# Output projections by a Strassen scheme over 12 of 16 row tiles, in a two-layer hybrid encoder step on one core

## The chip, the core and the metric

The kernel runs on one core of a Trainium2 chip. Times are device microseconds of one execution. A core has five engines with queues of their own, worked off in order: TensorE (PE, matmuls; PEld is its weight load), VectorE (DVE), ScalarE (ACT), GpSimd (POOL) and SyncE (SP, which issues DMAs here). An instruction waits on semaphores until what it reads is written and what it overwrites has been read.

## The reference, cut to what matters

Two layers over 640 tokens (512 of a prompt, 8 x 16 of samples) with 2048 channels, all in float32:

```
h = rms_norm(x, norm_g);  z = h @ w_in
y_a = conv group (4 tiles of 128 channels), y_b = window attention (8 tiles), y_c = memory attention (4 tiles)
y = concat([y_a, y_b, y_c]) @ w_out          # 2048 x 2048, the change is here
x = x + y
```

A final RMSNorm follows the second layer.

## The kernel before, in words

Activations lie transposed: a row tile is 128 channels by 640 tokens, and there are 16 of them (`NK`). The tokens stand in two halves of 320 (`HT`). `R` [128, 16, 640] holds the outputs of the three groups, then the layer's result; rows 0 to 7 are the window attention, 8 to 11 the memory attention, 12 to 15 the convolution. `HL` [128, 32, 640] holds the matmuls' right-hand side as a high part (first 16 rows) and a low part (last 16).

A float32 product is made of three passes of a faster type: `split` writes the high part by a ScalarE copy (L126) and the low part by a VectorE subtraction (L127); a product is high x high, high x low and low x high. `x_split` does the same for a layer's input with the norm's factor in it (L129, L130). `proj` (L726 to L739) computes a column tile of a projection: 16 k tiles, three passes, two halves, 96 matmuls of 128x320 (L735) into two PSUM banks `z`. Its weights come in four chunks of 512 columns; `wprep` loads a chunk on SP's queue, splits it at high priority, and has three buffers each of `wr`, `wh` and `wl`.

A layer is 38 column tiles of w_in with the three groups' work between them, then the split of `R` into `HL` (`HL<-R`), then the column tiles of w_out: `proj`, an addition of the residual (L907), in layer 0 a store of the result to `x1d`, and `add_sq`, a square on ScalarE (L242) and a sum on VectorE (L243) for the next norm. Layer 0 does all 16 columns so. Layer 1 does 14; the last two stand in a tail of their own, in parts of 384 and 256 tokens (L931), with their weights split ahead of it into `wh` and into attention buffers (`g`, `u`).

The order on each queue is made ahead of time by a list scheduler from the program, with weight work at high priority; pools of buffers in SBUF and PSUM set which instruction waits for which reader. PSUM has two `z` tiles and four `a` tiles.

## Time and profile before

| | |
|---|---|
| Runs | 1870.96, 1871.5, 1872.04 us (median 1871.5) |
| The profiled execution's own time | 1871.64 us |
| Its span | 1869.9 us |
| TensorE busy | 1849.1 us, 99% |
| VectorE busy | 1113.7 us, 60% |
| ScalarE busy | 744.0 us, 40% |
| GpSimd busy | 159.9 us, 9% |
| Out-projections | layer 0 from 751.42 to 976.7, layer 1 from 1625.72 to 1822.84 us |

The span runs from the first to the last instruction. Busy shares are means over stages; which wait ends last is read stage by stage. TensorE's matmuls overlap, so a matmul's own duration (about 310 ns for 128x320) is longer than the distance to the next.

### The profile page before, as it was taken

How to read it: one execution, taken by the hardware profiler on the slowest of the kernel's cores; microseconds unless marked ns; L12 is line 12 of the kernel's file. 1: busy time of each engine (PE TensorE's matmuls, PEld its weight loads, DVE VectorE, ACT ScalarE, POOL GpSimd, SP SyncE). 2: the span in 40 equal slices, each digit the busy share in tenths (PEclk: the TensorE clock that was granted, in tenths of full speed). 3: DMA queues.
4: the chain of work that ended last, by engine and by line, in shares of the span. 5: the costliest groups of instructions: out<-in, count | busy, mean ns of one | idle time of the engine just before them, and what ended most of it. 6: DMA issues, size and time to landing. Idle time of an engine off the chain costs nothing.

```text
span 1869.9 us, 32663 instructions
## 1 busy us (share of the span) xinstructions
PE 1849.1 (99%) x12846; PEld 1802.2 (96%) x12846; DVE 1113.7 (60%) x2385; ACT 744.0 (40%) x1578; POOL 159.9 (9%) x349
## 2 busy tenths in 40 slices
PE   8999999999999999999999999999999999999996
PEld 8899999999998999999999999999999989999996
DVE  7859998567554445432256999756755434623235
ACT  7831224657553334322242222555654324522221
POOL 1121210000000010000021000000000010000000
PEclk9999999999999999999999999999999999999998
DMA  8844532222222343344343332222232243333333
GB/s 281 288 120 105 124 108 76 72 69 67 81 83 73 105 160 102 116 130 119 119 121 91 80 85 81 74 69 71 65 89 80 75 135 125 115 96 102 97 102 134
DMA packets 92394, 200.36 MB, mean 107 GB/s; under 512 B 12256, under 2 KB 17296, under 8 KB 92208
## 3 DMA queue, kind: packets, MB, share of 16 engines
q1 hardware_dynamic: 72592, 139.75, 24.7%
q0 software_dynamic: 17184, 55.63, 10.0%
q10 hardware_dynamic: 2464, 2.88, 0.4%
q8 instruction: 101, 1.65, 0.4%
q14 instruction: 53, 0.43, 0.1%
...
## 4 chain that ended last, share of the span: by engine, by line
PE 98%; DVE 1%; DMA 0%; ACT 0%; issue 0%; DVEq 0%; POOLq 0%
PE z L735 80%; PE a L266 3%; PE z L289 2%; PE a L483 2%; PE a L526 2%; PE a L463 2%; PE z L931 1%; DVE R L964 1%; PE a L514 1%; PE a L622 1%; PE a L661 1%; PE a L648 1%; PE a L557 1%; PE a L517 1%; PE a L595 1%; PE a L690 1%
## 5 line engine op out<-in xcount | busy, mean ns | idle before, releaser
L735 PE MATMUL z<-HL,wh 128*128 128x320 f32 x6784 | 1308.8, 311 | 0.0
L735 PEld LDWEIGHTS z<-HL,wh 128*128 128x128 f32 x6784 | 1068.8, 188 | 8.8 <-issue 5.7
L735 PE MATMUL z<-HL,wl 128*128 128x320 f32 x3392 | 788.4, 311 | 0.0
L126 ACT ACTIVATE wh<-wr 128x512 fp32r<-128x512 f32 x431 | 271.7, 631 | 761.4 <-PE z L735 682.4
L735 PEld LDWEIGHTS z<-HL,wl 128*128 128x128 f32 x3392 | 569.4, 188 | 3.5 <-issue 1.6
L127 DVE TENSOR_TENSOR wl<-wr,wh 128x512 fp32r<-128x512 f32 x431 | 297.0, 689 | 380.2 <-ACT wh L126 367.6
L411 DVE SCALAR_TENSOR_TENSOR R<-R,sm 128x128 f32<-128x128 f32 (+1 forms) x480 | 235.0, 548 | 0.1
L907 DVE TENSOR_TENSOR R<-z,zt 128x640 f32<-128x640 f32 x30 | 24.8, 825 | 70.5 <-PE z L735 70.5
L127 DVE TENSOR_TENSOR g<-a,g 128x512 fp32r<-128x512 f32 x80 | 49.5, 634 | 27.2 <-ACT g L126 26.6
L487 DVE CUSTOM_DVE_ANT_0 g<-a,R 128x256 f32<-128x256 f32 (+1 forms) x128 | 46.4, 388 | 23.4 <-PE a L483 20.0
L499 ACT ACTIVATE g<-g,sml 128x256 f32<-128x256 f32 (+1 forms) x128 | 59.8, 470 | 0.0
L126 ACT ACTIVATE g<-a 128x512 fp32r<-128x512 f32 x80 | 42.3, 552 | 42.3 <-PE a L517 29.9
L506 ACT ACTIVATE g<-g,sml 128x256 f32<-128x256 f32 (+1 forms) x128 | 51.4, 473 | 3.9 <-DVE sml L502 3.9
L471 POOL DMA_DIRECT2D R<-brep x32 | 17.4, 543 | 406.2 <-DVE sml L487 166.9
L266 PE MATMUL a<-HL,wh 128*128 128x256 f32 x256 | 42.9, 289 | 6.0 <-ACT HL L129 6.0
L127 DVE TENSOR_TENSOR wl<-u,wh 128x512 fp32r<-128x512 f32 x60 | 40.6, 687 | 6.2 <-ACT wh L126 6.1
L126 ACT ACTIVATE wh<-u 128x512 fp32r<-128x512 f32 x60 | 37.5, 627 | 15.7 <-PE z L289 8.0
L266 PEld LDWEIGHTS a<-HL,wh 128*128 128x128 f32 x256 | 37.6, 195 | 6.3 <-ACT HL L129 6.0
L289 PE MATMUL z<-wh,HL 128*128 128x512 f32 x128 | 41.1, 399 | 0.6 <-ACT wh L126 0.6
L531 ACT ACTIVATE g<-a 64x512 f32<-64x512 f32 x32 | 19.0, 594 | 41.0 <-PE a L526 40.7
L532 DVE TENSOR_TENSOR g<-a,g 64x512 f32<-64x512 f32 x32 | 22.0, 687 | 20.0 <-ACT g L531 19.6
L463 PE MATMUL a<-u,g 128*128 128x320 f32 x192 | 33.8, 312 | 0.0
...
## 6 DMA issues: line engine op xcount, KB each, us to landing
wr<-w_in SPq DMA_DIRECT2D x304, 256.0 KB, 2.7
wr<-w_out SPq DMA_DIRECT2D x128, 256.0 KB, 2.7
...
R<-xT SPq DMA_DIRECT2D x16, 320.0 KB, 5.3
zt<-xT POOLq DMA_DIRECT2D x16, 320.0 KB, 4.6
```

What stands on the lines that cost most here:

```text
L126: a = ac.activation(hi, raw, AF.Copy)
L127: v = ve.tensor_tensor(out=lo, in0=raw, in1=hi.bitcast(F32), op=ALU.subtract)
L266: pe.matmul(ps[ct][:, :256], w[:, ws], mslot(l, k, lo), start=k == 0 and n == 0, stop=k == NK - 1 and n == 2,)
L289: pe.matmul(psv[:, m, :], mslot(l, k, lo)[:, ms], w, start=k == 0 and n == 0, stop=k == NK - 1 and n == 2,)
L411: ve.scalar_tensor_tensor(out=o, in0=x, scalar=w, in1=o, op0=ALU.mult, op1=ALU.add)
L463: pe.matmul(ps[:, :HT], w[:, ws], x[:, k, :], start=n == 0, stop=n == 11)
L483: pe.matmul(ps[:, j, c0:256], q[:, p * P:(p + 1) * P], kk[n][h][:, (p - 1) * P + c0:(p + 1) * P], start=n == 0, stop=n == 1,)
L487: ve.tensor_tensor_reduce(out=x[:, j, c0:], in0=ps[:, j, c0:], in1=bt[:, c0:], scale=1.0, scalar=-3.0e38, op0=ALU.add, op1=ALU.max, accum_ ...
L499: ac.activation(x, x, AF.Exp, bias=ng[:, p:p + 1], accum_out=sm_[:, p:p + 1])
L506: ac.activation(x, x, AF.Copy, scale=rd[:, p:p + 1])
L526: pe.matmul(po[:, os], V[h][:, v, :], p[:, ms], start=v == 0 and n == 0, stop=v == 3 and n == 1, skip_group_check=True,)
L735: pe.matmul(ps[:, s, :HT], w[:, ws], HL[:, lo * NK + k, s * HT:(s + 1) * HT], start=k == 0 and n == 0, stop=k == NK - 1 and n == 2,)
```

## The change

In the out-projections, columns 0 and 1 stay as they were. The others go in pairs (j, j+1): seven pairs in layer 0 (j = 2 to 14), six in layer 1 (j = 2 to 12); the two columns of the tail stay plain. In a pair the four first row tiles (`KS`) are multiplied plainly. The other twelve are two blocks of six, `KB` (rows 4 to 9) and `KA` (rows 10 to 15); with the two halves of tokens (`TA`, `TB`) and the two columns they are a 2x2 block product, done by Winograd's form of Strassen's scheme with seven products instead of eight. A product is 6 k tiles in three passes, 18 matmuls (`s_mm`).

`combos` makes the combinations of the activations once a layer, by eight subtractions of 960 elements in `R`, and splits them into T2, T3, T4 and, over `HL`'s rows `KA` of the second half, T1. `s_pair` makes the combinations of the weights for each pair on VectorE (`s1`, `s2`, a21 becoming a11 - a21, a12 becoming a12 - s2), splits each product's weights (two buffers `sh`, `sl` of 768, six raw ones `sr`) and adds the products from the PSUM accumulators `X`, `Dd` and `z` into `R`, where the residual has been loaded (`add_to`). A pair's products come in the order p1, a12, a12 - s2, the plain part of both columns, p7, p6, p4, p5; in the last pair of layer 1 the plain part, with a12 and a12 - s2 ahead of it, comes last.

The buffers: `wr`, `wh`, `wl` and the attention buffers are in pools (`wp`, `at`) that are given back before the out-projections, whose pools (`tt`, `sw`) lie in the same memory; the tail has one more (`tw`) with weight buffers for all eight chunks. In layer 1 `R[:, KA, TB]` is stored to DRAM (`y12d`) before `combos`, and read back and split again over T1 for the tail, whose two plain columns need it. The host lays w_out out so that a column's weights are one row of 2048 a partition.

```
+    def s_mm(out, w, x, start, stop):
+        n = w[0].shape[-1] // P
+        for k in range(n):
+            for i, (a, b) in enumerate(passes(w, x)):
+                pe.matmul(
+                    out, a[:, k * P:(k + 1) * P], b[:, k, :], start=start and k == 0 and i == 0,
+                    stop=stop and k == n - 1 and i == 2, skip_group_check=True,
+                )
...
+    def combos():
...
+        T[1] = hl(KA, TB)
+        gs = [(slice(KA.start + g, KA.start + g + 3), slice(KB.start + g, KB.start + g + 3)) for g in (0, 3)]
+        for a, b in gs:
+            sub(R[:, a, TA], R[:, a, TB], R[:, a, TA])
+            sub(R[:, a, TB], R[:, b, TB], R[:, a, TB])
+            sub(R[:, b, TB], R[:, b, TB], R[:, a, TA])
+        place = {1: (0, TA), 2: (1, TB), 3: (0, TB), 4: (1, TA)}
+        for n in (3, 2, 4, 1):
+            for g, ab in enumerate(gs):
+                i, cs = place[n]
+                if n == 4:
+                    sub(R[:, ab[1], TA], R[:, ab[1], TA], R[:, ab[1], TB])
+                ks = slice(3 * g, 3 * g + 3)
+                split(R[:, ab[i], cs], None, T[n][0][:, ks, :], T[n][1][:, ks, :])
...
+    def s_pair(l, j1, T, resid, early):
...
+        for j in (j1, j2):
+            gp.dma_start(R[:, j, :], resid[j])
+        X, Dd = pa()[:, :HT], pa()[:, :HT]
+        with tc.high_priority():
+            a11 = s_load(wj[0][:, cut[0]])
+            a21 = s_load(wj[1][:, cut[0]])
+            a22 = s_load(wj[1][:, cut[1]])
+            a12 = s_load(wj[0][:, cut[1]])
+            p1 = s_split(a11)
+            s1, s2 = s_raw(), s_raw()
+            ve.tensor_tensor(out=s1, in0=a21, in1=a22, op=ALU.add)
+            sub(s2, s1, a11)
+            sub(a21, a11, a21)
+        s_mm(X, p1, hl(KA, TA), True, True)
+        add_to(R[:, j1, TA], X)
+
+        def plain():
+            z = pz()
+            with tc.high_priority():
+                w = s_split(a12)
+            s_mm(z[:, 0, :HT], w, hl(KB, TA), True, False)
+            with tc.high_priority():
+                sub(a12, a12, s2)
+                w = s_split(a12)
+            s_mm(z[:, 1, :HT], w, hl(KB, TB), True, False)
+            w = s_prep(wj[0][:, cut[2]])
+            for s, cs in enumerate((TA, TB)):
+                s_mm(z[:, s, :HT], w, hl(KS, cs), False, True)
+            add_to(half(R[:, j1, :]), z[:, :, :HT])
+            z = pz()
+            w = s_prep(wj[1][:, cut[2]])
+            for s, cs in enumerate((TA, TB)):
+                s_mm(z[:, s, :HT], w, hl(KS, cs), True, True)
+            add_to(half(R[:, j2, :]), z[:, :, :HT])
...
+        p6 = (s2, 2, X, False, [(j2, TA)])
+        p7 = (a21, 3, Dd, True, [(j2, TB)])
+        p5 = (s1, 1, X, False, [(j2, TB), (j1, TB)])
+        p4 = (a22, 4, Dd, False, [(j2, TA)])
...
+        phase_pools("tt", "sw")
         for k in range(NK):
             split(R[:, k, :], None, HL[:, k, :], HL[:, NK + k, :])
+        if l == L - 1:
+            gp.dma_start(y12d, R[:, KA, TB])
...
-    W = [(None, None)] * 3 + [(g2, g2)] * 4 + [(u5, None)]
-    W = [wprep(A["w_out"][L - 1, NK - 2 + p // 4, p % 4], *W[p]) for p in range(8)]
...
+    y12 = tl([P, 6, HT], "y12", 1, F32, cur["tw"])
+    with tc.high_priority():
+        gp.dma_start(y12, y12d)
```

In the order below, a row is a line of the program, the operation, what is written and read, and the size. VectorE where the attention of layer 0 ends, before: `wl` are low parts of weight chunks, `HL<-R` low parts of the activations; L701 is the memory attention's last product, L710 the eviction of the last w_in column.

```order
L127 TENSOR_TENSOR HL<-R,HL 128x640
L127 TENSOR_TENSOR wl_8524<-wr_8521,wh_8523 128x512
L127 TENSOR_TENSOR HL<-R,HL 128x640 x3
L652 TENSOR_TENSOR R<-a_8171,R 128x2x256
L127 TENSOR_TENSOR HL<-R,HL 128x640
L127 TENSOR_TENSOR wl_8554<-wr_8551,wh_8553 128x512
L127 TENSOR_TENSOR HL<-R,HL 128x640
L701 TENSOR_TENSOR R<-a_8354,R 128x2x64
L127 TENSOR_TENSOR HL<-R,HL 128x640 x2
L710 SCALAR_TENSOR_TENSOR zt_8480<-z_8358,rstd 128x640
L127 TENSOR_TENSOR HL<-R,HL 128x640
L127 TENSOR_TENSOR wl_8584<-wr_8581,wh_8583 128x512
```

`wl_8524`, `wl_8554` and `wl_8584` are the first three chunks of w_out. The same place after the change; `sl` are low parts of w_out's chunks, L720 is the eviction, L775 a subtraction of `combos`, L1025 and L1026 the last gate.

```order
L137 TENSOR_TENSOR HL<-R,HL 128x640 x2
L712 TENSOR_TENSOR R<-a_8361,R 128x2x64
L137 TENSOR_TENSOR HL<-R,HL 128x640 x2
L720 SCALAR_TENSOR_TENSOR zt_8487<-z_8365,rstd_1245 128x640
L137 TENSOR_TENSOR HL<-R,HL 128x640
L137 TENSOR_TENSOR sl_8539<-sr_8536,sh_8538 128x512
L137 TENSOR_TENSOR sl_8569<-sr_8566,sh_8568 128x512
L775 TENSOR_TENSOR R<-R 128x3x320
L1025 SCALAR_TENSOR_TENSOR zt_8487<-zt_8486,zt_8487 128x640
L775 TENSOR_TENSOR R<-R 128x3x320
L1026 TENSOR_TENSOR R<-R,zt_8487 128x640
L137 TENSOR_TENSOR sl_8599<-sr_8596,sh_8598 128x512
```

The first w_out chunk, `sl_8539`, has moved behind the eviction and the HL splits around it.

VectorE over one column in the middle of layer 0's out-projection, before:

```order
L907 TENSOR_TENSOR R<-z_8774,zt_8772 128x640
L127 TENSOR_TENSOR wl_8966<-wr_8963,wh_8965 128x512
L243 TENSOR_TENSOR w_1326_8517<-w_1326_8517,w_1370_8897 128x640
L127 TENSOR_TENSOR wl_8996<-wr_8993,wh_8995 128x512
L127 TENSOR_TENSOR wl_9034<-wr_9031,wh_9033 128x512
L127 TENSOR_TENSOR wl_9064<-wr_9061,wh_9063 128x512
L907 TENSOR_TENSOR R<-z_8902,zt_8900 128x640
```

After, from the end of one pair to the first plain addition of the next: `a_9319` is the last pair's `X`, `a_9569` this pair's, `sr_9577` a12, `sr_9584` s2, and L253 the sum of squares.

```order
L813 TENSOR_TENSOR R<-a_9319,R 128x320 x2
L137 TENSOR_TENSOR sl_9609<-sr_9577,sh_9608 128x768
L253 TENSOR_TENSOR w_1331_8532<-w_1331_8532,w_1461_9560 128x640
L775 TENSOR_TENSOR sr_9577<-sr_9577,sr_9584 128x768
L813 TENSOR_TENSOR R<-a_9569,R 128x320
L253 TENSOR_TENSOR w_1331_8532<-w_1331_8532,w_1462_9564 128x640
L137 TENSOR_TENSOR sl_9632<-sr_9577,sh_9631 128x768
L137 TENSOR_TENSOR sl_9656<-sr_9653,sh_9655 128x512
L137 TENSOR_TENSOR sl_9688<-sr_9685,sh_9687 128x512
L813 TENSOR_TENSOR R<-z_9607,R 128x640
```

Where a column had a weight split, an addition and a sum, the splits now stand between additions, sums and a subtraction that makes the next split's input.

VectorE where the out-projection of layer 0 ends and w_in of layer 1 begins, before: L130 are the low parts of layer 1's input, `wl` the first column of w_in.

```order
L130 SCALAR_TENSOR_TENSOR HL<-R,sm,HL 128x640 x4
L127 TENSOR_TENSOR wl_10601<-wr_10598,wh_10600 128x512
L130 SCALAR_TENSOR_TENSOR HL<-R,sm,HL 128x640 x4
L127 TENSOR_TENSOR wl_10631<-wr_10628,wh_10630 128x512
L130 SCALAR_TENSOR_TENSOR HL<-R,sm,HL 128x640 x2
L907 TENSOR_TENSOR R<-z_10438,zt_10436 128x640
L130 SCALAR_TENSOR_TENSOR HL<-R,sm,HL 128x640 x2
L127 TENSOR_TENSOR wl_10661<-wr_10658,wh_10660 128x512
```

After, the same place; `sl_10536` is the weight of p5, the last product, and `a_10319` its accumulator.

```order
L137 TENSOR_TENSOR sl_10536<-sr_10333,sh_10535 128x768
L813 TENSOR_TENSOR R<-a_10320,R 128x320
L140 SCALAR_TENSOR_TENSOR HL<-R,sm,HL 128x640 x2
L813 TENSOR_TENSOR R<-a_10319,R 128x320 x2
L140 SCALAR_TENSOR_TENSOR HL<-R,sm,HL 128x640 x2
L137 TENSOR_TENSOR wl_10613<-wr_10610,wh_10612 128x512
L137 TENSOR_TENSOR wl_10643<-wr_10640,wh_10642 128x512
L137 TENSOR_TENSOR wl_10673<-wr_10670,wh_10672 128x512
```

The first chunks of w_in, which stood among the HL splits ahead of the last addition, stand behind p5's additions and two more HL splits.

## Rows read from the trace of the kernel before

**Rows 1.** The page's first part: busy time of each engine, its share of the span, instructions.

```profile
PE 1849.1 (99%) x12846; PEld 1802.2 (96%) x12846; DVE 1113.7 (60%) x2385; ACT 744.0 (40%) x1578; POOL 159.9 (9%) x349
```

**Rows 2.** The waits of TensorE: engine, tile and line, what it waited for, microseconds in total, times, the longest.

```profile
PE a L266 <- ACT HL L129: 6.0, 1, 6.0
PE a L200 <- DVE sml L186: 2.5, 1, 2.5
PE a L210 <- ACT w L956: 1.1, 1, 1.1
PE z L289 <- ACT wh L126: 0.6, 1, 0.6
```

**Rows 3.** The page's chain that ended last, by engine and by line, in shares of the span.

```profile
PE 98%; DVE 1%; DMA 0%; ACT 0%; issue 0%; DVEq 0%; POOLq 0%
PE z L735 80%; PE a L266 3%; PE z L289 2%; PE a L483 2%; PE a L526 2%; PE a L463 2%; PE z L931 1%; DVE R L964 1%; PE a L514 1%; PE a L622 1%; PE a L661 1%; PE a L648 1%; PE a L557 1%; PE a L517 1%; PE a L595 1%; PE a L690 1%
```

**Rows 4.** Busy time by engine in a stretch of layer 0's out-projection: PE, PEld, DVE, ACT, POOL busy microseconds (instructions), TensorE's granted clock, share of the DMA engines, GB/s.

```profile
760.00:960.00 200.00, 200.00 (x1366) 200.00 (x1365) 60.08 (x84) 46.42 (x71) 15.06 (x28) 1.00 0.40 122
```

**Rows 5.** The timeline of VectorE in the same stage: start, microseconds, line, operation, idle time before it and what ended it. The additions of two successive columns.

```profile
850.18 0.82 DVE L907 TENSOR_TENSOR R<-z,zt 128x640 f32<-128x640 f32 x1 [2.46 <-PE z L735]
...
864.26 0.82 DVE L907 TENSOR_TENSOR R<-z,zt 128x640 f32<-128x640 f32 x1 [2.46 <-PE z L735]
```

**Rows 6.** The timeline of TensorE, with the pointwise projection of a convolution tile (L463) among w_in's matmuls, and where a column of the out-projection begins.

```profile
508.36 1.63 PE L463 MATMUL a<-u,g 128*128 128x320 f32 x10
509.83 0.75 PE L735 MATMUL z<-HL,wh 128*128 128x320 f32 x4
...
849.98 0.75 PE L735 MATMUL z<-HL,wh 128*128 128x320 f32 x4
```

**Rows 7.** Groups of instructions by line and shape over the whole span: count, busy microseconds, mean nanoseconds of one, idle time before them and what ended it.

```profile
L127 DVE TENSOR_TENSOR wl<-wr,wh 128x512 fp32r<-128x512 f32 x431 | 297.0, 689 | 380.2 <-ACT wh L126 367.6 <-PE z L735 9.7 <-issue 1.2
...
L243 DVE TENSOR_TENSOR w<-w,w 128x640 f32<-128x640 f32 x34 | 28.0, 825 | 5.7 <-ACT w L242 5.6
...
L426 DVE SCALAR_TENSOR_TENSOR R<-a,R 128x320 f32<-128x320 f32 x16 | 6.9, 485 | 3.9 <-PE a L191 3.7
...
L127 DVE TENSOR_TENSOR u<-R,u 128x1280 fp32r<-128x1280 f32 x4 | 6.0, 1493 | 1.7 <-PE a L463 1.6
...
L126 ACT ACTIVATE wh<-wr 128x512 fp32r<-128x512 f32 x431 | 271.7, 631 | 761.4 <-PE z L735 682.4 <-issue 48.3 <-DVE R L411 14.3
...
L242 ACT ACTIVATE w<-R 128x640 f32<-128x640 f32 x34 | 25.2, 740 | 15.6 <-DVE R L907 13.9 <-DVE w L243 1.5
```

**Rows 8.** The timelines of TensorE and of ScalarE where layer 0's out-projection begins.

```profile
751.42 0.75 PE L735 MATMUL z<-HL,wh 128*128 128x320 f32 x4
...
750.74 1.37 ACT L126 ACTIVATE HL<-R 128x640 fp32r<-128x640 f32 x2 [0.37 <-PE z L735]
752.01 0.61 ACT L126 ACTIVATE wh<-wr 128x512 fp32r<-128x512 f32 x1
```

**Rows 9.** The timeline of VectorE in the same place.

```profile
751.51 0.83 DVE L127 TENSOR_TENSOR HL<-R,HL 128x640 fp32r<-128x640 f32 x1 [0.23 <-ACT HL L126]
752.25 0.82 DVE L710 SCALAR_TENSOR_TENSOR zt<-z,rstd 128x640 f32<-128x640 f32 x1
752.99 0.81 DVE L127 TENSOR_TENSOR HL<-R,HL 128x640 fp32r<-128x640 f32 x1
753.72 0.68 DVE L127 TENSOR_TENSOR wl<-wr,wh 128x512 fp32r<-128x512 f32 x1
```

**Rows 10.** DMA issues: what is written and read, queue, count, KB each, median microseconds from issue to landing.

```profile
x1d<-R POOLq DMA_DIRECT2D x16, 320.0 KB, 3.3
...
yT<-R SPq DMA_DIRECT2D x4, 384.0 KB, 3.2
...
yT<-R SPq DMA_DIRECT2D x4, 256.0 KB, 2.5
...
o_vold<-cv POOLq DMA_DIRECT2D x1, 896.0 KB, 13.0
```

**Rows 11.** The timelines of VectorE and of ScalarE shortly before layer 1's w_in begins.

```profile
972.09 3.27 DVE L130 SCALAR_TENSOR_TENSOR HL<-R,sm,HL 128x640 fp32r<-128x640 f32 x4
...
973.83 3.02 ACT L129 ACTIVATE HL<-R,sm 128x640 fp32r<-128x640 f32 x4
```

**Rows 12.** The timelines of ScalarE and of VectorE where the tail begins.

```profile
1815.76 0.63 ACT L126 ACTIVATE wh<-wr 128x512 fp32r<-128x512 f32 x1 [2.89 <-PE z L735]
...
1823.04 0.82 DVE L907 TENSOR_TENSOR R<-z,zt 128x640 f32<-128x640 f32 x1 [1.79 <-PE z L735]
```

**Rows 13.** The timeline of TensorE at the start of the kernel; from 5.96 to 9.56 there are 17 matmuls, from 9.56 to 10.41 seven.

```profile
5.96 1.44 PE L266 MATMUL a<-HL,wh 128*128 128x256 f32 x5 [5.96 <-ACT HL L129]
...
8.68 1.04 PE L266 MATMUL a<-HL,wh 128*128 128x256 f32 x5
9.56 0.29 PE L266 MATMUL a<-HL,wl 128*128 128x256 f32 x1
...
10.41 0.76 PE L266 MATMUL a<-HL,wh 128*128 128x256 f32 x5
```

**Rows 14.** Busy time in two stretches of the tail, columns as in rows 4.

```profile
1850.00:1856.00 6.00, 4.42 (x38) 4.25 (x36) 5.93 (x15) 0.42 (x1) 0.00 (x0) 0.99 0.91 324
1856.00:1862.00 6.00, 1.22 (x4) 0.93 (x4) 5.69 (x20) 0.00 (x0) 0.00 (x0) 0.50 0.64 227
```

More of the change, by code (lines that the diff above doesn't have):

```diff
@@ L68, in build, with phase_pools @@
     dr = pool("dr", bass.MemoryType.DRAM)
-    uid, last = [0], {}
+    uid, last, cur = [0], {}, {}
+    phase = ctx.enter_context(ExitStack())
+    home = {t: "wp" for t in ("wr", "wh", "wl", "rstd")}
+    home |= {t: "at" for t in ("g2", "qh", "u5", "kc", "kh", "kl", "mh", "ml", "vh", "vl", "cqs")}
+    def phase_pools(*names):
+        phase.close()
+        for n in names:
+            uid[0] += 1
+            cur[n] = phase.enter_context(tc.tile_pool(name=f"{n}{uid[0]}", bufs=1, reuse_waits="tile"))
     def tl(shape, tag, bufs, dt=F32, pl=None):
         uid[0] += 1
-        return (pl or sb).tile(shape, dt, tag=tag, name=f"{tag}_{uid[0]}", bufs=bufs)
+        pl = pl or (cur[home[tag]] if tag in home else sb)
+        return pl.tile(shape, dt, tag=tag, name=f"{tag}_{uid[0]}", bufs=bufs)
     def w25():
@@ L301, in build @@
     mraw = []
+    phase_pools("wp", "at")
     def load_mem(j):
@@ L712, in evac2 @@
     def evac2(ps, outp, outs, scale=1.0):
+        rs3 = half(cur["rstd"])
         ve.scalar_tensor_tensor(
@@ L739, in proj, with s_raw, s_split, s_load @@
         return ps
+    KS, KB, KA = slice(0, 4), slice(4, 10), slice(10, 16)
+    TA, TB = slice(0, HT), slice(HT, TOK)
+    def s_raw(n=6):
+        return tl([P, 768], "sr", 6, F32, cur["sw"])[:, :n * P]
+    def s_split(raw):
+        n = raw.shape[-1]
+        hi = tl([P, 768], "sh", 2, F32R, cur["sw"])[:, :n]
+        lo = tl([P, 768], "sl", 2, F32R, cur["sw"])[:, :n]
+        split(raw, None, hi, lo)
+        return hi, lo
+    def s_load(src):
+        raw = s_raw(src.shape[-1] // P)
+        load(raw, src)
+        return raw
@@ new lines, in s_prep, with sub, hl @@
+    def s_prep(src):
+        with tc.high_priority():
+            return s_split(s_load(src))
+    def sub(out, a, b):
+        ve.tensor_tensor(out=out, in0=a, in1=b, op=ALU.subtract)
+    def hl(ks, cs):
+        return HL[:, ks, cs], HL[:, slice(NK + ks.start, NK + ks.stop), cs]
+    def combos():
+        T = {}
+        tt = [
+            (tl([P, 6, HT], f"th{n}", 1, F32R, cur["tt"]), tl([P, 6, HT], f"tl{n}", 1, F32R, cur["tt"]))
+            for n in (2, 3, 4)
+        ]
+        T[2], T[3], T[4] = tt
+        T[1] = hl(KA, TB)
[12 more added lines that the diff above has]
+                split(R[:, ab[i], cs], None, T[n][0][:, ks, :], T[n][1][:, ks, :])
+        return T
@@ new lines, in s_mm, with add_to, mixed @@
+    def s_mm(out, w, x, start, stop):
[6 more added lines that the diff above has]
+                )
+    def add_to(out, ps):
+        ve.tensor_tensor(out=out, in0=ps, in1=out, op=ALU.add)
+    def s_pair(l, j1, T, resid, early):
+        j2 = j1 + 1
+        wj = [A["w_out"][l, j1], A["w_out"][l, j2]]
+        cut = [slice(ks.start * P, ks.stop * P) for ks in (KA, KB, KS)]
+        for j in (j1, j2):
[31 more added lines that the diff above has]
+            add_to(half(R[:, j2, :]), z[:, :, :HT])
+        def mixed(raw, n, out, start, dst):
+            with tc.high_priority():
+                w = s_split(raw)
+            s_mm(out, w, T[n], start, True)
+            for j, cs in dst:
+                add_to(R[:, j, cs], out)
+        p6 = (s2, 2, X, False, [(j2, TA)])
+        p7 = (a21, 3, Dd, True, [(j2, TB)])
+        p5 = (s1, 1, X, False, [(j2, TB), (j1, TB)])
+        p4 = (a22, 4, Dd, False, [(j2, TA)])
+        if not early:
+            plain()
+        for a in (p7, p6, p4, p5):
+            mixed(*a)
+        if early:
+            plain()
```

56 lines of the change are left out of this document (43 added, 13 removed).

## The prediction

> **What bounds the kernel now.** I read the page's busy shares first: TensorE is busy 99% of the span, VectorE 60%, ScalarE 40% [rows 1]. Then the waits: in 1869.9 us TensorE waits four times, 10.2 us in all, none of them in the projections [rows 2]. The chain of waits says the same: 98% of it is TensorE, 80% the one matmul line of the projections [rows 3]. So the end is set by the number of matmuls times their pace, and an edit gains what it takes off TensorE's queue, less what it makes TensorE wait. In the out-projection stage the other engines have room: in a stretch of 200 us TensorE is busy for all of it, VectorE for 60 us, ScalarE for 46 [rows 4].
>
> The pace comes from the VectorE timeline: the residual additions of successive columns start 14.08 us apart [rows 5], and a column has 96 matmuls, so 146.7 ns for one of 128x320.
>
> **What is removed.** Thirteen pairs of columns (seven in layer 0, six in layer 1) go from 192 matmuls to seven products of 18 and 48 plain ones, 174. So 13 x 18 = 234 matmuls fall, and the built order of TensorE has just that many fewer. At 146.7 ns: **34.3 us**. A new product uses each weight block twice (high part), then its low block once, where `proj` uses them four times and twice. The pointwise projection, L463, already has the new pattern: ten of them take 1.47 us to the next start, 147 ns each [rows 6]. So the pace stays; by that row's difference 1638 matmuls would cost half a microsecond at most, which I leave out.
>
> **What is added on VectorE and ScalarE.** Sizes of 768 and 960 elements do not occur before. VectorE takes 689 ns for 512, 825 for 640, 1493 for 1280 [rows 7], about 1.05 ns an element, so 0.96 us for 768 and 1.16 for 960; back to back 640 ones start 0.735 us apart [rows 9], 0.09 under their length, so 0.87 and 1.07. ScalarE: 0.63 for 512, 0.74 for 640 [rows 7], so 0.85 for 768. A pair has on VectorE seven low parts of 768 and two of 512, four additions or subtractions of 768, six additions of 320, two of 640 and two of squares: some 16.5 us in 25.5 us of TensorE. It fits as a sum; what counts is each slot.
>
> **Inside a pair (2.0 us in all).** The split weights have two buffers, so a product's weights can be split only when the product two before has ended, and are wanted 2.64 us later (the low part 0.29 us after that, as the third matmul). High and low part take 0.85 + 0.96, so 0.8 to 1.1 us is left for other VectorE work. The tight slot is the third product, a12 less s2. Its subtraction stands on VectorE behind two additions of the last pair's p5, the low part of a12 and a square sum. From the pair's start, with an addition beginning 0.20 us after TensorE's last matmul [rows 5, 6]: 0.20, two additions of 0.42, low part 0.87, squares 0.73, subtraction 0.87, the addition of p1 0.42, squares 0.73, low part 0.96: ready at 5.62. It is wanted at 5.28 + 0.29 = 5.57. With every operation at its full length (0.49, 0.96, 0.83) instead of overlapped the end is 6.19, 0.62 late. Bounds 0 and 0.62 a pair; I take 0.15, near the overlapped sum, since rows 9 show the operations overlapped: 13 x 0.15 = 2.0 us (0 to 8).
>
> **Attention to out-projection (2.4 us, twice).** Before, the three weight buffers carry over: the first out-projection chunk is split while w_in still runs, and TensorE goes from one to the other without a gap at 751.42 (seven columns ahead of the boundary at 849.98 [rows 6, 8]). After, the chunks come into a new pool that lies where attention buffers were; in the built order their splits stand behind the last HL split on ScalarE, and on VectorE behind the gate's eviction and one HL split more. ScalarE has there two HL splits from 750.74, and is free at 752.01 [rows 8]; the high part is ready at 752.64, 1.22 us after 751.42. VectorE has an HL split at 751.51, the eviction at 752.25, an HL split at 752.99 and is free at 753.72 [rows 9]; the low part is there at 754.41, and the fifth matmul wants it at 752.64 + 0.59: 1.2 more. Sum 2.4; 1.2 if the low part comes in time after all, 3.1 if VectorE does one HL split more ahead of it. The combinations (eight subtractions and eight low parts of 960, 17 us) lie beside 28 us of two plain columns; by the same counting their weight splits come just in time: 0.3 us.
>
> **The store in layer 1 (2.5 us).** There the second quarter is stored (983 KB) ahead of the combinations. The store waits for the last gate, about 6.2 us into the stage, and a subtraction that overwrites its source waits for it to land; behind that on VectorE stand the splits of the second column's chunks 0 and 1. With landing L after the gate, the chunk 1 split ends at 15.9 + L and is wanted at 20.6: lost are L - 4.7, and 0.4 in the chunk behind. Stores from SBUF take 2.5 us for 256 KB and 3.2 for 384 [rows 10]: 0.7 for each 128 KB, so 6.3 for 960 KB, with 0.5 to issue 6.9, which gives 2.5. Bounds: 0 at L = 3.3, the store of x1d's 320 KB, and 8.7 at L = 13, a DRAM copy of 896 KB [rows 10].
>
> By the Trainium skill's page "DMA: Bandwidth & Descriptors", section "Anatomy of one DMA — SWDGE (gpsimd) path", such a transfer takes about 2.0 us and its bytes at 436 GB/s: an estimate of 4.3 us, by which this term would be 0.4. For x1d's 320 KB it gives 2.8 where the row has 3.3.
>
> **Out-projection to w_in of layer 1 (3.0 us).** p5 reads the HL rows that layer 1's splits must overwrite, so ScalarE does four of them (0.73 apart [rows 11]) as p5's k tiles end, from 2.0 us before the end, and only then the first w_in weights: high part ready at +1.55. VectorE has the two additions of p5 from +0.42, two HL low parts (0.80 apart [rows 11]) and then the weights: low part at +3.6, wanted at 1.55 + 0.59. So 3.0; 1.55 if the low part is in time, 3.8 with one HL split more ahead. Before, TensorE had no wait there [rows 2].
>
> **To the tail (2.9 us).** The new splits stand behind the last pair's eviction and two squares: 0.20 + 0.82, square 0.74, split 0.63 with 0.1 overlapped: high part at +2.35; the low part, behind a square sum on VectorE, 0.55 late. 2.35 if it is in time, 3.6 with one square more ahead. Before, the splits for the tail begin at 1815.76, as buffers come free, 7 us ahead of its first matmul, which starts 0.20 before the addition at 1823.04 [rows 12].
>
> **The sum.** 34.3 - (2.0 + 2.4 + 2.4 + 0.3 + 2.5 + 3.0 + 2.9 = 15.5) = 18.8 us. The profiled execution took 1871.64 us (span 1869.9 and 1.7 around it), the median of the runs 1871.5, so 0.1 below: **1852.7 us**.
>
> **Rivals.** (a) All terms at their low ends (2 x 1.2 + 0.3 + 1.55 + 2.35 = 6.6): 1843.8; for it speaks that scheduled orders kept TensorE fed everywhere before, against it that the named splits stand behind work that ends after the boundary. (b) **The clock falls in the new gaps.** After the idle 5.96 us at the start, the first 17 matmuls take 3.60 us, 212 ns each, the later ones 0.12 us [rows 13]: 1.55 us lost, the lower of the clock's levels, 1.2 GHz. In the tail the granted clock reads 0.50 after waits of 1.1 and 2.5 us among a few small matmuls [rows 2, 14]. If each of the four boundaries did that, 6.2 us: 1858.9; with the store at its high bound, 1865. Against it: at the boundaries my gaps come in two parts of 1 to 2 us, between dense matmuls. The Trainium skill's page "TensorE: Matmul & The Clock Gate", section "Why this matters for your kernels", says to leave no idle gaps between bursts of matmuls, since the clock then drops back; the start agrees, though the clock may have been low before it. (c) **Slower: two buffers do not hide the split.** Each product's weights then come late behind VectorE's other work, in all 9 slots of a pair. The gain is used up at 18.8 / 117 = 0.16 us a product, and it is slower by 0.2% from 0.19. If each slot had its operations at full length plus one addition of 0.49, it is about 0.25 late: 117 x 0.25 less the 2.0 already counted: 1880. For it: three slots have under 0.5 us to spare; against: rows 9 show the overlap, and VectorE has a third of the time free. (d) The change does nothing there: excluded by the count of matmuls, unless the pace changes.
>
> **How the numbers follow.** Forecast 1852.7 with its near terms, 1848 to 1858: 0.55. (a) 1838 to 1848: 0.15. (b), or a slow store, 1858 to 1866: 0.17. Pairs late by 1 to 1.6 us, 1866 to 1875: 0.06. (c): 0.07. The range takes (b) and the upper part of (a): 1843 to 1866. A measurement here can tell about 0.2%, 3.7 us, so faster ends at 1867.8: 0.89; same 0.04; slower 0.07.
>
> **What would show it.** Right: 234 matmuls fewer at 146 to 147 ns in the pairs; TensorE waiting for ScalarE and VectorE splits at the four boundaries, 2 to 5 us each; a VectorE subtraction waiting for the y12d store. Wrong: waits of TensorE on the low parts in every product (c), granted clock under 1.00 in the pairs or matmuls of 0.29 us behind a boundary (b), or boundaries without a gap (a).

## The result, and the profile after

The changed kernel took 1861.68 us, the median of four runs (1858.35 to 1861.93), beside 1871.64 of the kernel before (1870.96 to 1872.04): a ratio of 0.9943, 95% interval 0.9926 to 0.9960. The forecast was 1852.7, so the sign held, the time lies in the range (1843 to 1866), in the part that rival (b) or a slow store was to fill, and half of the gain did not come. The four runs lie 3.6 us apart, those of before 1.1.

The profiled execution took 1861.93 us, its span is 1860.1, 9.8 us under the span of before. The page's first part (columns as in [rows 1]): TensorE has the 234 matmuls fewer, VectorE 145 us more work, and TensorE's share has fallen from 99% to 98%.

```profile
PE 1825.3 (98%) x12612; PEld 1772.8 (95%) x12612; DVE 1258.2 (68%) x2562; ACT 789.3 (42%) x1609; POOL 160.8 (9%) x351
```

The windows of the five stages of the kernel after (columns as in [rows 4]): layer 0 to the end of its w_in, its out-projection, w_in of layer 1, its out-projection, the tail.

```profile
0.00:752.68 752.68, 745.13 (x5167) 716.60 (x5167) 511.70 (x1133) 352.75 (x769) 78.84 (x174) 1.00 0.41 120
752.68:964.85 212.17, 209.22 (x1412) 206.85 (x1410) 154.27 (x202) 84.20 (x110) 20.99 (x44) 1.00 0.38 123
964.85:1618.72 653.87, 651.30 (x4579) 632.67 (x4577) 431.96 (x985) 276.12 (x633) 52.17 (x117) 1.00 0.31 89
1618.72:1808.79 190.07, 184.75 (x1238) 182.73 (x1236) 130.19 (x169) 67.15 (x87) 8.84 (x16) 0.99 0.33 109
1808.79:1860.10 51.31, 34.88 (x224) 33.93 (x222) 30.12 (x74) 9.11 (x15) 0.00 (x0) 0.83 0.37 129
```

The same stages of the kernel before, cut at the same matmuls:

```profile
0.00:751.42 751.42, 744.83 (x5168) 716.50 (x5169) 513.28 (x1135) 353.06 (x771) 77.99 (x174) 1.00 0.39 119
751.42:976.70 225.28, 225.28 (x1539) 225.28 (x1538) 80.58 (x112) 64.01 (x98) 21.72 (x41) 1.00 0.41 122
976.70:1625.72 649.02, 649.02 (x4579) 630.95 (x4578) 430.50 (x983) 273.60 (x630) 51.58 (x118) 1.00 0.30 88
1625.72:1822.84 197.12, 197.12 (x1346) 197.12 (x1345) 63.35 (x88) 47.84 (x75) 8.07 (x15) 1.00 0.33 101
1822.84:1869.90 47.06, 32.81 (x224) 32.34 (x222) 25.99 (x69) 5.48 (x10) 0.54 (x1) 0.85 0.40 135
```

Stage by stage after is shorter by -1.3, 13.1, -4.9, 7.1 and -4.3 us. The out-projections lost 126 and 108 matmuls, 18.5 and 15.8 us at 146.7 ns, and kept 13.1 and 7.1 of it; three stages from which nothing was taken became longer. What filled them stands in TensorE's waits (after; columns as in [rows 2]; the three rows that answer to rows of before are left out):

```profile
PE z L746 <- DVE sl L137: 4.2, 3, 2.3
PE z L746 <- DVE wl L137: 2.7, 2, 1.6
...
PE z L1096 <- ACT xh L136: 2.3, 1, 2.3
PE z L746 <- ACT sh L136: 2.2, 2, 1.1
PE z L746 <- ACT wh L136: 1.4, 1, 1.4
...
PE a L807 <- DVE sl L137: 0.8, 1, 0.8
PE z L807 <- ACT sh L136: 0.5, 1, 0.5
PE z L807 <- DVE sl L137: 0.4, 1, 0.4
PE z L1096 <- DVE xl L137: 0.3, 1, 0.3
```

Most of them lie where the prediction put them: at the entries to the out-projections (`sh`, `sl` on line 746), to layer 1 (`wh`, `wl`), to the tail (`xh`, `xl`) and at the store (`sl`, 2.3). One `wl` wait (1.56) is in layer 0's w_in, and those on line 807 (1.7 in all) are in layer 0's last pair and layer 1's first. But a wait is not the whole price. TensorE's timeline of the kernel after, where layer 1's w_in begins:

```profile
964.70 0.31 PE L807 MATMUL a<-HL,sl 128*128 128x320 f32 x1
966.42 0.86 PE L746 MATMUL z<-HL,wh 128*128 128x320 f32 x4 [1.41 <-ACT wh L136]
968.44 0.56 PE L746 MATMUL z<-HL,wl 128*128 128x320 f32 x2 [1.16 <-DVE wl L137]
968.84 0.91 PE L746 MATMUL z<-HL,wh 128*128 128x320 f32 x4
...
971.68 1.21 PE L746 MATMUL z<-HL,wh 128*128 128x320 f32 x4
972.73 0.45 PE L746 MATMUL z<-HL,wl 128*128 128x320 f32 x2
```

From start to start, less 0.147 a matmul, the two gaps are 1.57 and 1.43 us, 3.0 together, as forecast. Then 16 matmuls from 968.84 to 972.73 take 3.89 us where 2.35 would do: 1.54 us more. The same stands behind the store's wait (12 matmuls from 1641.97 to 1645.24 in 3.27 us, 1.51 too many) and behind the entry to the tail (12 of 384 columns, 0.173 us each at full pace, from 1812.15 to 1815.90 in 3.75, 1.67 too many). The granted clock in these three stretches (windows of the kernel after, columns as in [rows 4]) is about half, the lower of its two levels, 1.2 GHz:

```profile
968.90:972.60 3.70, 3.70 (x17) 3.70 (x16) 3.69 (x6) 1.32 (x2) 3.66 (x8) 0.55 0.87 264
1642.00:1645.20 3.20, 3.20 (x12) 3.20 (x13) 3.20 (x4) 1.36 (x2) 0.00 (x0) 0.51 0.63 207
1812.20:1815.80 3.60, 3.60 (x12) 3.60 (x13) 3.23 (x4) 2.36 (x4) 0.00 (x0) 0.53 0.43 146
```

### The profile page after: what moved, and what is told of

It is laid out like the page before. It is cut to its first block, busy times and chain, and to the rows that moved or that the text cites. A ratio compares the mean times of both kernels' runs of the same rounds, so it can differ in the third digit from the quotient of the medians.

```text
span 1860.1 us, 32336 instructions
## 1 busy us (share of the span) xinstructions
PE 1825.3 (98%) x12612; PEld 1772.8 (95%) x12612; DVE 1258.2 (68%) x2562; ACT 789.3 (42%) x1609; POOL 160.8 (9%) x351
## 4 chain that ended last, share of the span: by engine, by line
PE 95%; DVE 2%; DMA 1%; issue 0%; ACT 0%; DVEq 0%; ACTq 0%; POOLq 0%
PE z L746 60%; PE a L807 9%; PE z L807 8%; PE a L276 3%; PE z L299 2%; PE a L494 2%; PE a L537 2%; PE a L474 2%; PE z L1096 1%; DVE R L1129 1%; PE a L525 1%; DMA wr<-w_in 1%; PE a L633 1%; PE a L672 1%; PE a L659 1%; PE a L568 1%
## 5 line engine op out<-in xcount | busy, mean ns | idle before, releaser
L746 PE MATMUL z<-HL,wh 128*128 128x320 f32 x4864 | 950.4, 312 | 1.4 <-ACT wh L136 1.4
L746 PEld LDWEIGHTS z<-HL,wh 128*128 128x128 f32 x4864 | 768.4, 188 | 10.5 <-issue 5.7
L746 PE MATMUL z<-HL,wl 128*128 128x320 f32 x2432 | 570.4, 312 | 2.7 <-DVE wl L137 2.7
L746 PEld LDWEIGHTS z<-HL,wl 128*128 128x128 f32 x2432 | 409.4, 188 | 6.5 <-DVE wl L137 3.3
L137 DVE TENSOR_TENSOR wl<-wr,wh 128x512 fp32r<-128x512 f32 x308 | 212.2, 690 | 184.6 <-ACT wh L136 172.2
L136 ACT ACTIVATE sh<-sr 128x768 fp32r<-128x768 f32 (+1 forms) x133 | 103.4, 780 | 221.0 <-PE z L807 92.0
L807 PE MATMUL z<-HL,sh 128*128 128x320 f32 x728 | 160.7, 309 | 0.5 <-ACT sh L136 0.5
L137 DVE TENSOR_TENSOR sl<-sr,sh 128x768 fp32r<-128x768 f32 (+1 forms) x133 | 115.6, 871 | 41.6 <-ACT sh L136 41.6
L807 PEld LDWEIGHTS z<-HL,sh 128*128 128x128 f32 x728 | 121.7, 188 | 0.8 <-ACT sh L136 0.8
L807 PE MATMUL z<-HL,sl 128*128 128x320 f32 x364 | 113.8, 313 | 0.6 <-DVE sl L137 0.4
```

Of the source, the lines that this page charges most:

```text
L136: a = ac.activation(hi, raw, AF.Copy)
L137: v = ve.tensor_tensor(out=lo, in0=raw, in1=hi.bitcast(F32), op=ALU.subtract)
L746: pe.matmul(ps[:, s, :HT], w[:, ws], HL[:, lo * NK + k, s * HT:(s + 1) * HT], start=k == 0 and n == 0, stop=k == NK - 1 and n == 2,)
L807: pe.matmul(out, a[:, k * P:(k + 1) * P], b[:, k, :], start=start and k == 0 and i == 0, stop=stop and k == n - 1 and i == 2, skip_group_c ...
```

## The experiments

Twelve runs, all beside the kernel before (1871.3 to 1872.0). The differences in the last column are to the second run of the changed kernel, e1.

| run | edit | median us (range) | ratio, 95% interval | to e1 |
|---|---|---|---|---|
| e1 | none | 1859.29 (1857.65 to 1863.70) | 0.9936, 0.9921 to 0.9950 | |
| e2 | new pools, old columns | 1893.65 (1893.18 to 1895.36) | 1.0117, 1.0102 to 1.0132 | +34.4 |
| e3 | no store | 1856.88 (1854.53 to 1857.87) | 0.9917, 0.9902 to 0.9932 | -2.4 |
| e4 | first column on old buffers | 1856.69 (1856.67 to 1859.39) | 0.9923, 0.9906 to 0.9939 | -2.6 |
| e5 | tail's pool shorter | 1856.63 (1855.99 to 1857.87) | 0.9922, 0.9905 to 0.9938 | -2.7 |
| e6 | plain products last in layer 0 | 1863.01 (1862.67 to 1863.39) | 0.9954, 0.9939 to 0.9969 | +3.7 |
| e7 | shared rows between the splits | 1858.30 (1856.68 to 1859.84) | 0.9928, 0.9914 to 0.9943 | -1.0 |
| e8 | cache copies later | 1864.30 (1863.02 to 1864.75) | 0.9960, 0.9945 to 0.9974 | +5.0 |
| e9 | halves stored from HL | 1851.14 (1849.99 to 1853.28) | 0.9891, 0.9877 to 0.9904 | -8.2 |
| e10 | one plain product last | 1861.73 (1861.44 to 1863.36) | 0.9948, 0.9934 to 0.9962 | +2.4 |
| e11 | all mendings | 1864.97 (1863.16 to 1866.34) | 0.9962, 0.9949 to 0.9976 | +5.7 |
| e12 | e9, e4, e7 in middle pairs | 1849.18 (1848.03 to 1850.06) | 0.9877, 0.9861 to 0.9894 | -10.1 |

**e1, the changed kernel again.**

> The changed kernel as it is, timed again beside the next three. Theory A: of the 34.3 us of matmuls saved, about 17 go into waits at the four stage boundaries, the store and the pairs, 4.7 into three stretches at half matmul pace behind the longest of these waits, 1.3 into the first layer's input projection, whose order is the same in both kernels. So 1861.7 again within 0.3, with a run near 1858.4 now and then when one or two of the last two kinds stay out. Rival: the loss beyond the waits was chance of that chip, then the median is near 1855 to 1858.

Neither theory has the median: 1859.29 lies between their ranges. The four runs spread over 6 us, where before spreads over 1.3. The profiled one, the slowest (1863.70), has the waits of the table above within a few tenths, and half pace after four of them instead of three. The fourth is the entry to layer 0's out-projection; windows around it, the kernel after first, then e1:

```profile
740.00:770.00 30.00, 27.98 (x206) 26.12 (x204) 27.07 (x35) 15.72 (x24) 3.63 (x7) 1.00 0.43 134
```

```profile
740.00:770.00 30.00, 27.98 (x196) 26.12 (x195) 26.18 (x35) 15.90 (x24) 2.42 (x5) 0.94 0.42 131
```

Both have the same two waits there, 1.10 and 0.92 us, and the same busy time; the clock fell in one. The spread fits falls of some 1.5 us each; differences below about 3 us between the variants are read from the traces here, not from medians.

**e2, the new pools with plain columns in all of them** (no pairs, combinations or store).

```diff
-        for j in list(range(2)) + list(range(2, done, 2)):
+        for j in range(done):
...
-                s_pair(l, j, T, resid, l == L - 1 and j + 2 == done)
```

> All columns plain again (the matmuls of the kernel before), no combinations and no store, but the buffers handed over as in the changed kernel. Theory A: the handing over alone costs the waits at the boundaries, 2.4 twice, about 2 into layer 1, 2.9 into the tail, and half pace behind one or two of them: 1871.6 + 9.7 + 1.5 to 3 = 1883 (1879 to 1886). Rival B: the losses come from the products (denser VectorE work, combinations), and the pools alone cost nothing: 1871 to 1873.

It lies 21.7 us above the kernel before. The columns keep their 14.08 us with two split buffers, so the pace is not it; it is at the boundaries and at 246 us, 14.2 us of waits, and half pace behind some.

```profile
PE z L746 <- ACT sh L136: 7.7, 2, 4.9
...
PE z L746 <- DVE wl L137: 2.9, 2, 1.6
...
PE z L1081 <- ACT xh L136: 2.3, 1, 2.3
```

The 1883 was too low by ten: there are 4.5 us more of waits than forecast, and half pace in four stretches (6.4 us in all, granted clock 0.50 to 0.53), not in one or two. Nor is e2 the pure price of the pools: without the combinations' pool the landing buffers lie over w_in's weight buffers, and ScalarE's timeline where layer 1's out-projection begins shows the raw weight late, not the order (its load is issued at 1640.55, after TensorE's last w_in matmul at 1638.7):

```profile
1643.17 0.63 ACT L136 ACTIVATE sh<-sr 128x512 fp32r<-128x512 f32 x1 [1.92 <-DMA sr<-w_out]
```

That e2 less e1 is 34.4 us and the matmuls' term 34.3 is then partly chance.

**e3, without the store** (what comes back for the tail is a part of `x1d` of the same size, so the tail computes with other values in six row blocks).

> The changed kernel without the store of R[:, KA, TB] to DRAM in layer 1; what is read back for the tail is another tensor of the same size, so the second half of the last two columns is wrong. Theory A: the wait behind the store (2.5 us) and the 12 matmuls at half pace after it (1.5) both go: 4.0 less than the changed kernel, 1857.7. Rival: half pace has another cause and stays, or the next late split takes the wait's place: 2.3 less or nothing, 1859.4 to 1861.7.

The store's wait is gone, and so are the waits on line 807 in layer 1's first pair (0.5 and 0.4 in the list above): these belong to the store too. In the kernel after, VectorE's timeline there shows the stall, and the list of issues its cause, 7.1 us of landing:

```profile
1628.95 0.69 DVE L137 TENSOR_TENSOR sl<-sr,sh 128x512 fp32r<-128x512 f32 x1 [0.92 <-ACT sh L136]
1632.41 2.23 DVE L775 TENSOR_TENSOR R<-R 128x960 f32<-128x960 f32 x2 [2.77 <-DMA y12d<-R]
1634.55 0.69 DVE L137 TENSOR_TENSOR sl<-sr,sh 128x512 fp32r<-128x512 f32 x1
```

```profile
y12d<-R POOLq DMA_DIRECT2D x1, 960.0 KB, 7.1
```

**e4, the first column on the old weight buffers**, pools changed behind it.

```diff
-        phase_pools("tt", "sw")
         for k in range(NK):
             split(R[:, k, :], None, HL[:, k, :], HL[:, NK + k, :])
+        ps0 = proj([A["w_out"][l, 0][:, c * 512:(c + 1) * 512] for c in range(4)])
+        phase_pools("tt", "sw")
...
```

> Column 0 of each out-projection takes its weights through the old buffers, and the new pools open after it. Theory A: its chunks are split ahead of the boundary as in the kernel before, so the waits of 2.4 us at both attention boundaries go; the order then has seven operations of the combinations ahead of column 1's third chunk, about 1.3 late in each layer: 4.9 - 2.6 = 2.3 less, 1859.4. Rival: the hand-over only moves to column 1's first chunk and nothing is won: 1861.7.

The waits at the entries are gone, 2 x 2.45 us, and the store's fell from 2.3 to 0.5; others of 1.7 (`sl`, layer 0's second column), 1.5 and 1.4 us (layer 1's first pair) took their place. In layer 0's second column VectorE does three low parts of the combinations in a row (3.29 us) ahead of the weight that TensorE wants. The time is 2.7 us under theory A's 1859.4: in the profiled run the clock falls at one place only behind a wait, at the entry to layer 1.

**e5, one number in the tail.** The tail's pool holds y12 (7,680 bytes a partition), `xr`, eight `xh` and eight `xl` of 2,048; with three `xr` that is 46,592, and the combinations' pool under it 46,080, so that 512 bytes reach into the pool of `sr`, `sh` and `sl`.

```diff
-            raw = tl([P, 512], "xr", 3, F32, cur["tw"])
+            raw = tl([P, 512], "xr", 2, F32, cur["tw"])
```

> One number: the tail's landing buffers xr are 2 instead of 3, so that its pool ends at 196,896 instead of 198,944 and no longer reaches 512 bytes into the pool of sr/sh/sl. Theory A (the first split of a new pool is set late in the order because its pool touches one that is still in use, and that late place is the whole of the 3.0 us at the entry to the tail): the waits 'z L1096 <- ACT xh' (2.3) and '<- DVE xl' (0.3 to 0.6) vanish, and with them the half pace behind them (1.1 to 1.6 us); time 1855.3 (1853 to 1857.5) where the changed kernel again gave 1859.3. Rival (the raw weight or the stored combination lands late, which order cannot mend): the wait of 2 to 3 us stays at the same place, 1858.5 to 1861.

No wait on line 1096 is left. ScalarE's timeline says why: in the kernel after, the first `xh` stands behind the two squares of the last pair:

```profile
1806.33 0.74 ACT L252 ACTIVATE w<-R 128x640 f32<-128x640 f32 x1 [3.89 <-DVE R L813]
1809.90 0.74 ACT L252 ACTIVATE w<-R 128x640 f32<-128x640 f32 x1 [2.83 <-DVE R L813]
1810.54 1.14 ACT L136 ACTIVATE xh<-xr 128x512 fp32r<-128x512 f32 x2
```

ScalarE is idle for 3.9 and 2.8 us there, with the raw weight landed since 1794.2 (issued at 1791.2, 3.0 us to land): it waits for squares that nobody needs yet. In e5 the two `xh` stand ahead of the last pair's last three `sh` in the built order. Theory A holds: order, not data.

**e6, both plain products of layer 0's last pair behind the combinations.**

```diff
-                s_pair(l, j, T, resid, l == L - 1 and j + 2 == done)
+                s_pair(l, j, T, resid, j + 2 == done)
```

> In layer 0 too the last pair runs its four combination products first and its plain ones last, so that the combinations' pool is free one product earlier and the first two w_in weights of layer 1 stand ahead of the last out-projection weights in ACT's and DVE's order. Theory A (order, not data): 'z L746 <- ACT wh' 1.4 and '<- DVE wl' 1.2 to 1.6 vanish at the change from layer 0 to layer 1, with the half pace behind them (1.6 to 1.8 us): 1855 (1852.5 to 1857.5). Rival (layer 1's first column must wait for the splits of the residual into HL, which now have less cover): a wait of the same size with HL as its tile in the same place, 1858 to 1861.

Theory A missed, and the rival's waits on HL are there, but small (0.3 and 0.4 us). `ACT wh` is gone, but 3.9 us of waits (0.85 and 3.04, start to start) appear in the last pair: ScalarE does layer 1's residual and w_in first, and then the weights that the pair still wants:

```profile
951.00 2.98 ACT L139 ACTIVATE HL<-R,sm 128x640 fp32r<-128x640 f32 x4
953.88 1.66 ACT L136 ACTIVATE wh<-wr 128x512 fp32r<-128x512 f32 x3
955.45 1.35 ACT L136 ACTIVATE sh<-sr 128x768 fp32r<-128x768 f32 x2
```

And in layer 1's second column, which the edit does not touch, three `sl` waits (1.7, 1.1, 0.8) stand in place of one: the order there was re-made too.

**e7, the shared rows' product between a12 and a12 less s2.**

```diff
             s_mm(z[:, 0, :HT], w, hl(KB, TA), True, False)
+            w = s_prep(wj[0][:, cut[2]])
+            for s, cs in enumerate((TA, TB)):
+                s_mm(z[:, s, :HT], w, hl(KS, cs), s == 1, s == 0)
             with tc.high_priority():
                 sub(a12, a12, s2)
...
```

> In each of the 13 pairs the plain product of the shared rows (KS) is moved between a12's product and that of a12-s2, which gives DVE's subtraction and the two splits 48 more matmuls (some 7 us) of cover. Theory A (the 0.18 us per pair, read at 840.95 and 866.65, is the low half of a12-s2 coming late): 13 x 0.18 = 2.3 us gone, 1857.0 (1855 to 1859). Rival (the slip is the price of two buffers and moves to the next weight): the slip stays at 0.15 to 0.2 in another line of the same pair, 1859 (1857.5 to 1861).

TensorE's timeline, one matmul and the same one a pair later, first of the kernel after (25.70 us apart), then of e7 (25.52, which is 174 x 0.1467):

```profile
840.95 0.42 PE L807 MATMUL z<-HL,sl 128*128 128x320 f32 x1
...
866.65 0.42 PE L807 MATMUL z<-HL,sl 128*128 128x320 f32 x1
```

```profile
839.57 0.46 PE L807 MATMUL z<-HL,sh 128*128 128x320 f32 x2
...
865.09 0.46 PE L807 MATMUL z<-HL,sh 128*128 128x320 f32 x2
```

So the 0.18 us a pair are the late low part, as theory A has it. But the first and the last pair of layer 0 got new waits (1.3 and 2.8 us where e1 has 0.8 and 0.9), which used up most of the 2.3.

**e8, the two cache copies four columns later.**

```diff
-            if l == 0 and n in (8, 9):
+            if l == 0 and n in (12, 13):
...
```

> The two copies of the old caches (896 KB each, on POOL's queue) are issued four columns later in layer 0. Nothing of the change under study is touched. Theory A (the 1.2 to 1.6 us that PE waits at 246 us in all five runs of the changed kernel's kind is a w_in weight landing behind these copies and the 16 of the bias table): the wait goes, 1857.9 (1856 to 1859.5). Rival (the bias table's copies alone do it, or the weight is late for another reason): the wait of 1.2 to 1.6 stays at 245 to 248, 1859.3.

Theory A fell: the wait at 245 us stays, 2.06 us, and the w_in weight on which it hangs still lands late, beside the copies of the bias table alone. It is one issued at 224.8 to 226.8 us; ScalarE and VectorE work in order and stand until it is there, and VectorE then needs some 6.1 us, before as after, to the low part that TensorE wants. ScalarE's timeline, before and after, at the split of that weight:

```profile
238.42 0.63 ACT L126 ACTIVATE wh<-wr 128x512 fp32r<-128x512 f32 x1 [6.73 <-PE z L735]
```

```profile
239.43 0.63 ACT L136 ACTIVATE wh<-wr 128x512 fp32r<-128x512 f32 x1 [8.36 <-DMA wr<-w_in]
```

The order of TensorE, ScalarE and VectorE up to there is the same in all fourteen traces, and TensorE's wait follows this one landing: none where it took 12.2 (before, e7) or 12.4 us (e11), 0.21 at 12.5 (e10), 0.77 at 13.1 (e5), 1.28 at 13.6 (e1), 1.56 at 13.9 (after), 2.06 at 14.1 (e8). The profiled run (1864.01) has four falls of the clock (granted 0.98 in 200 to 300 us, 0.94 in 740 to 770, 0.95 in 950 to 985, 0.91 in 1800 to 1820), as many as e1's slowest (1863.70). That all four runs lie there is not explained by the edit.

**e9, split halves stored straight from HL**, two transfers, and brought back into HL.

```diff
-            gp.dma_start(y12d, R[:, KA, TB])
+            for d, t in zip(y12d, hl(KA, TB)):
+                gp.dma_start(d, t)
...
-        gp.dma_start(y12, y12d)
-        b12 = hl(KA, TB)
-        for g in (0, 3):
-            ks = slice(g, g + 3)
-            split(y12[:, ks, :], None, b12[0][:, ks, :], b12[1][:, ks, :])
+        for d, t in zip(y12d, hl(KA, TB)):
+            gp.dma_start(t, d)
```

> The six row blocks that the tail needs back are stored as their split halves, straight from HL, and come back into HL; the copy of R that the combinations' subtractions had to wait for is gone, and the tail splits nothing again. Two transfers of 960 KB in place of one, each way. Theory A (the 2.3 us at the third column of layer 1 is DVE's in-order stall behind 'DMA y12d <- R'): that wait goes, as it did where the store was left out (1856.9), and the entry to the tail keeps its 3.0 or loses it, since the pool there is 15,360 bytes shorter and no longer touches the pool in use: 1856.9 to 1854, middle 1855. Rival (the transfers' bulk, 1.92 MB each way, costs more than the wait): HL comes back late, a wait of 3 to 8 us on HL in the tail, 1860 to 1866.

Theory A in its waits, and faster than its range (1851.14 against 1854 to 1856.9). The subtractions may overwrite R at once; the tail's pool is 7,680 bytes shorter (not the 15,360 of the expectation) and its splits come early, as in e5. Both waits are gone, with the half pace behind them. The waits that are left, beside those that the kernel before has:

```profile
PE z L746 <- ACT sh L136: 2.2, 2, 1.1
PE z L746 <- DVE sl L137: 1.9, 2, 0.9
PE z L746 <- DVE wl L137: 1.6, 2, 1.2
PE z L746 <- ACT wh L136: 1.4, 1, 1.4
...
PE a L807 <- DVE sl L137: 0.8, 1, 0.8
PE z L807 <- DVE sl L137: 0.3, 2, 0.2
```

The bulk, 960 KB twice each way (6.3 and 6.6 us out, 5.8 and 9.6 back), costs TensorE nothing: no wait on HL there.

**e10, one plain product last.**

```diff
         for a in (p7, p6, p4, p5):
             mixed(*a)
...
+        if early:
+            plain2()
```

> In layer 0's last pair only the last plain product (24 + 24/1 matmuls of the second column's shared rows, some 3.5 us) is put behind the four combination products, so that the first w_in weights of layer 1 have the last combination product and it as cover, and no out-projection weight but one stands behind them. Theory A (the entry to layer 1 needs a few us of work between the last reader of the combinations and the first w_in product, and nothing else): 'ACT wh' 1.4 and 'DVE wl' 1.2 there go, with the half pace behind them, and no new wait of over 0.9 us appears before 965 us: 1855 (1853 to 1857.5). Rival (as when both plain products went last, the waits move into the pair): 2 to 4 us of waits at 950 to 965, 1858 to 1863.

The rival in another shape: `wh` comes in time, and now the residual's own splits are late.

```profile
PE z L746 <- DVE HL L140: 2.6, 1, 2.6
...
PE z L746 <- ACT HL L139: 1.0, 1, 1.0
```

3.6 us of waits in place of 2.6, and in layer 1's second column the same three `sl` waits as in e6 (1.4, 1.1, 0.8) in place of one; the 0.8 us in layer 0's last pair is gone. The entry to layer 1 has 16 HL splits, and those of the blocks that the last products read can't start before these end. The waits at the entry alone came down to 1.0 us in e6, at the price of 3.9 in the pair ahead; no edit tried gives the last pair and the entry together less than the some 4 us of the changed kernel.

**e11, all of it**, with the combinations held behind the second column's last-but-one weight.

> All the mendings together: first column on the old weight buffers, combinations held back behind the last-but-one weight split of the second column, shared-row product between the two splits of the first column's second block, halves stored from HL, layer 0's last product behind the combinations. Theory A (the changed kernel's loss against the matmuls that it saves is these waits and the half pace behind them, and each is a matter of order): the out-projection stages run at 0.1467 us per matmul of 320 columns throughout, 2.4 + 2.4 + 2.5 + 3.0 + 3.0 + 2.3 = 15.6 us of waits gone and 2 to 3 falls of the clock of 1.8 us each: 1859.3 - 15.6 - 1.0 to - 5.4 = 1838 to 1843, allowing for 3 us of small waits that stay: 1838 to 1846, middle 1842. Rival (DVE and ACT have too little slack there, and the waits only move): 1849 to 1856.

The rival, and worse. With the combinations held back, which was not run alone, VectorE does them in the first pair, with the pair's weights among them; from w_in's last matmul to the end of the first pair TensorE loses some 9.6 and 8.1 us against its pace in the two layers, where e1 loses 5.4 and 8.0. The entry to layer 1 has e10's 3.6 us of waits again.

```profile
PE z L809 <- DVE sl L137: 10.1, 6, 3.3
```

**e12, what had worked alone and meets at different places.**

> Split halves stored from HL (1851.1 alone), the first out-projection column on the old weight buffers, and the shared-row product between the two splits in the four middle pairs of each layer only, so that the first and last pairs keep their order. Theory A (each of these removed its own wait when it stood alone, and they meet at different places): 8 x 0.18 = 1.4 us in the pairs and 0.9 us in the first columns of each layer, 1851.1 - 1.4 - 1.8 = 1847.9, and 1.8 less where the clock no longer falls at 750 us: 1845.5 to 1849.5. Rival (the order of ACT and DVE is re-made around each edit, so that gains of single edits don't add, as they didn't with all of them together): new waits of 2 us or more in the second column or the first pair, 1851 to 1856.

1849.18, 12.5 us faster than the changed kernel's first measurement and 22.8 faster than before; in the profiled run the clock falls at one place, at the entry to layer 1, and 25.52 us is the period of the first three of the four middle pairs that were changed. Theory A at the upper end of its range (1849.5), with one wait of the rival's kind (`sl`, 1.7 us, second column, both layers).

## Why the prediction was half right

The sum of the profiled execution, term by term, start to start from TensorE's rows:

| term | forecast | measured |
|---|---|---|
| 234 matmuls at 146.7 ns | -34.3 | -34.3 |
| inside a pair, 13 x | 2.0 | 2.2 (12 x 0.18, none in layer 1's last) |
| attention to out-projection, twice | 4.8 | 4.9 (1.26 + 1.19 each) |
| combinations; first and last pairs | 0.3 | 2.7 (0.34, 0.94, 1.39) |
| store | 2.5 | 2.5 |
| out-projection to w_in | 3.0 | 3.0 |
| to the tail | 2.9 | 3.0 |
| half pace behind three waits | none | 4.7 |
| w_in of layer 0, same order as before | none | 1.3 |
| sum | -18.8 | -10.0 (spans: -9.8) |

- **The pace stayed.** The pair's period in e7 is 174 matmuls at 146.7 ns; rivals (c) and (d) are out.
- **The slots were right.** Five of the six priced waits are within 0.3 us, three of them in both their parts (high part late, then low part late). They come from which instruction stands ahead of which in the built order and the length of each: e4 and e5 take the waits at their places away without taking work away, e6 moves one, and e3 and e9 show that the store's wait hangs on its landing.
- **The store's landing was right** (6.9 against 7.1; 5.8 to 7.1 in the eight traces that have this store), by the rows of smaller stores; the lag that the prediction worked out from it would by its own figures be 2.6, not 2.5. The Trainium skill's page "DMA: Bandwidth & Descriptors", section "Anatomy of one DMA — SWDGE (gpsimd) path", makes it an estimate of 4.3 us; the 7.1 us of the trace disagree. What was missed is its second effect, 1.4 us in the first pair behind it (e3, e9): VectorE was still behind there. That, and 0.94 in layer 0's last pair, where VectorE does two low parts of layer 1's HL (954.53 to 956.2) ahead of its weight, are 2.3 of the 2.4 us by which the term of the combinations fell short.
- **The step that failed is rival (b)**, by how it was used. The forecast had the price (1.55 a place; measured 1.54, 1.51, 1.67) and gave it, together with a slow store, a chance of 0.17, as one event at all four places or none, since the gaps came "in two parts of 1 to 2 us, between dense matmuls". In the run it happened at three of five places and in e1 at four, and in the traces of the variants, where they have the same waits, less often: 22 of 40 places in all (entry to layer 0's out-projection 7 of 9, to layer 1's 0 of 9, to layer 1 7 of 9, store 2 of 5, tail 6 of 8). So it belonged into the sum as an expected cost; with this share, known only now, 5 places x 1.55 x 0.55 are some 4 us, where the run had 4.7. The Trainium skill's page "TensorE: Matmul & The Clock Gate", section "Why this matters for your kernels", says to leave no long idle gaps between bursts; in these traces shorter ones, of 0.9 to 2.3 us, were enough, though not each time.
- **1.3 us came from a place that the change does not touch**, a w_in weight that lands beside the bias table's copies. TensorE waits for it 0.5 to 2.1 us in ten of the thirteen traces of new kernels, and the length of this one landing sets the wait (e8). It is not the cache copies. Why it lands in 12.2 us in one execution and 14.1 in another stays open, and so does whether the kernel before, of which there is one trace, escapes as a rule.
- **Open as well**: what decides whether the clock falls at a given wait. It is not the wait's length alone: the two out-projections begin with the same two waits of 1.1 and 0.9 us, and the clock fell behind them in seven of nine traces in layer 0 and in none in layer 1.
